# Three main steps instead of two behind each small product in the mixer of a two-layer RWKV and pooling trunk

## The chip, the cores and the metric

The kernel runs on one core of one Trainium2 chip. The metric is the device time of one execution in microseconds (us), as the median of the runs shown. A profile of one further execution gives every instruction's start and duration on each engine: PE (TensorE, matrix products), DVE (VectorE), ACT (ScalarE), POOL (GpSimd) and SP (SyncE, which here only issues transfers).

## The reference

A prompt of 256 tokens and a sample group of 8 x 4 tokens (288 columns in all) pass through two layers that share all weights. Each layer is an FFN, a mixer and a second FFN. Cut to what matters:

```
for l in range(2):
    x = x + 0.5 * gate * swiglu(norm(x))                  # FFN, 1024 -> 2 x 2816 -> 1024
    p = u @ w_in[l]                                       # 19 column tiles of 128
    ya, state = rwkv7(p[:, :1824], ...)                   # S = S*w + (S a) b + v k ; y = S r ; group norm, gate
    yb = pool(p[:, 1824:], windows 2, 4, 8, 16) @ w_pool  # causal means less the input, one product for each window
    merged = sig(u @ w_gate_a) * (ya @ w_br_a) + sig(u @ w_gate_b) * (yb @ w_br_b)
    x = x + gate * (merged @ w_out)
    x = x + 0.5 * gate * swiglu(norm(x))                  # second FFN
y = final_norm(x)
```

The recurrence of the prompt is computed in chunks of 64 tokens: products of all token pairs inside a chunk ("scores"), the solution of a triangular system, and four chunk states one after the other. The 8 samples bring their own states, which are read, used and written back.

## The kernel before

Every large product runs in float32 precision as three passes of a rounded format: `mm3` (L244) multiplies the high part of the weights with the high and the low part of the activations, and the low part of the weights with the high part. One pass is a 128x128 weight block against 288 columns. For four weight blocks at a time ACT writes the high part `wh` (L225) and DVE the low part `wl` (L226); four such strips of `wh` and `wl` are held. All passes of `mm3` are tied to each other in the order of the code.

The mixer (`mixer`, from L623) has two streams of work on PE. The first are the **main passes**: `main_ops` goes through the column tiles of the list `MAIN` (the input projection `in`, the gate `ga` for pooling's branch), then pooling's branch product `bb` and the second half of `ga`. It is a generator: one **step** is two weight blocks, six passes. There are 22 x 4 steps for `MAIN`, 8 x 2 for `bb` and 8 x 4 for `ga`, 136 in all. The second stream are the **small products** of the recurrence, which wait for DVE and ACT between one another. `add` puts a small product into a queue with `WEAVE` steps behind it, and `fill()` takes the next number of `PLAN` and pops that many entries; where the queue is empty it makes plain steps:

```
def add(*items):
    for f in items:
        queue.extend((f,) + WEAVE * (step,))
def fill(n=None):
    for _ in range(next(plan, 2) if n is None else n):
        (queue.popleft() if queue else step)()
```

The mixer calls `fill()` once for each number of `PLAN`, in this order: seven times up to the scores (products L906, masked on DVE in L910); then a queue of 13 small products is added (`bonus`, eight transpositions into token order, `values`, `ak_v`) and `fill()` is called four times around the triangular system, whose DVE part ends in the tile `Tc` (L1172) and whose first product is L1179; the rest of the queue is emptied. Then nine products of the samples are added (among them `smp_state`, L1042, four times: each reads 256 KB of state into the one buffer of tag `O0` through a transfer on ACT's queue, and multiplies it, L1048), and `fill()` is called twice for each of the four chunks. In the second chunk eleven more are added: `spread_bonus` and `out_gate` twice each, `outputs(0)`, `smp_last(0)`, `smp_yt`, `transposed(0)`, `smp_last(1)`, `(2)`, `(3)`. `smp_last` (L1144) reads a state into the buffer `O0` again (ACT's queue), adds a product (L1152) to it on DVE (L1154), scales it on POOL (L1155) and writes it out on SP's queue. After the chunks come `outputs(1)`, a `fill()`, the rest of the queue, and `transposed(1)`: four transpositions on PE (L1238) and four DVE operations (L1141, L1142). The result `xv` is then split into `yah` (ACT, L522) and `yal` (DVE, L523) for four tiles with a `fill()` behind each, which are plain steps; `need(99)` makes the steps that are left. Then comes the product `ba`, whose first column tile needs all of `yah` and `yal`.

Pooling: `pooled` builds `dd` (its last operation is L695) on DVE, and `pool_out` (L704) multiplies it by the pooling weights (L706) and splits the result (`ybh` on ACT, `ybl` on DVE, L709). Each `dd` has one of two buffers. `pool_out` and the main passes take their PSUM tiles from the same three, `psmm`; the other small products take theirs from four others, `pswk`.

When the program is built, the instructions of each engine are put into a fixed order by priority (the order of the code, with a lead of 75 for the weights and some main results) and by when their inputs are reckoned to be ready. So the order on PE need not be that of the queue: where a small product is not ready, main passes that stand later in the code come first. It keeps the order in which the tiles of one PSUM pool are taken.

Of the kernel before, what the change touches and what calls it, by code (L numbers as in the profile page):

```python
# [27 lines left out]
KD = 8  # L28
# [37 lines left out]
TOK = (0, P, NT - P)  # L66
SLOT = 8
PRIO = 75
WEAVE = 2
PLAN = (1, 0, 0, 11, 1, 15, 12, 16, 5, 6, 2, 0, 10, 12, 2, 2, 1, 8, 13, 1, 2, 8, 4, 2, 3, 0, 5, 1, 1, 7)  # L70
FIRST = 3
RMS = {0: 0.25, 1: 0.15, 2: 0.25}
SPREAD = {0: 0.45, 1: 0.4, 2: 0.45}
# [115 lines left out]
class Kernel:  # L189
# [433 lines left out]
    def mixer(self, l):  # L623
# [7 lines left out]
        def tl(shape, tag, name=None, dt=F32, bufs=1):  # L631
            return pl.tile(shape, dt, tag=tag, name=name or tag, bufs=bufs)

        def f4(tag, name=None, dt=F32):
            return tl([P, HP, NT], tag, name, dt)
# [68 lines left out]
        def pool_out(g, dd):  # L704
            ps = self.ps_mm()
            T.matmul(ps[:, :NT], wpl[:, g, :], dd, start=True, stop=True)  # L706
            sc = self.par(l, "pool_scale", g)
            S.activation(out=ybh[:, g, :], in_=ps[:, :NT], func=AF.Copy, scale=sc)
            V.scalar_tensor_tensor(out=ybl[:, g, :], in0=ps[:, :NT], scalar=sc, in1=ybh[:, g, :].bitcast(F32),  # L709
                                   op0=ALU.mult, op1=ALU.subtract)  # L710

        dds = {}

        def project(m, ps):
            name, i = IN_TILES[m]
            if name == "la":
                shifted(i, ps, xla)
                S.activation(out=xla[0:64, :], in_=xla[0:64, :], func=AF.Tanh)
            elif name in "krv":
                shifted(i, ps, {"k": xk, "r": xr, "v": xv}[name][:, i % 4, :])  # L720
            elif name == "gl":
                shifted(i, ps, sgl[:, i - 13, :])
                S.activation(out=sgl[:, i - 13, :], in_=sgl[:, i - 13, :], func=AF.Sigmoid)
            else:
                dds[i - 15] = pooled(i - 15, ps)

        def project_pre(m, ps):
            p = p0[:, m % KD, :]
            c = self.scaled(ps, p, V)
            V.tensor_scalar(p[:, :TP], p[:, :TP], c, None, op0=ALU.add)  # L730
            project(m, p)

        def strip(name, m, n=KD, xh=None, xl=None, w=NT):
            xh, xl = (self.uh, self.ul) if xh is None else (xh, xl)
            ps = self.ps_mm()
            for k in range(n):
                self.mm3(ps[:, :w], (name, l, 0, m, k), xh[:, k, :], xl[:, k, :], k == 0, k == n - 1)
                if k % 2:
                    yield ps
# [3 lines left out]
        def main_ops():  # L743

            for n, (name, m) in enumerate(MAIN):
                pre = name == "in" and m < PRE_M
                for ps in strip(name, m, xh=self.vh, xl=self.vl, w=NV) if pre else strip(name, m):
                    yield n
                if (name, m) == ("in", PRE_M - 1):
                    self.v_cm.__exit__(None, None, None)  # L750
                with tc.high_priority(offset=PRIO):
                    if pre:
                        project_pre(m, ps)
                    elif name == "in":
                        project(m, ps)
                    else:
                        S.activation(out=t2s[0][:, m - KD, :], in_=ps[:, :NT], func=AF.Sigmoid,
                                     bias=self.par(l, "b_gate", m))
                if name == "in" and m == 14:
                    nc.sync.dma_start(out=self.io["o_shift"][l], in_=sho)  # L760
                if name == "in" and m == 14:
                    t2s.append(tl([P, KD, NT], "t2"))
                if name == "ga":
                    if m - KD - 2 in dds:
                        pool_out(m - KD - 2, dds[m - KD - 2])
                    self.mod_step()
            at_bb = len(MAIN)
            for m in range(KD):
                for ps in strip("bb", m, 4, ybh, ybl):
                    yield at_bb  # L770
                with tc.high_priority(offset=PRIO):
                    V.tensor_tensor(out=t2s[0][:, m, :], in0=t2s[0][:, m, :], in1=ps[:, :NT], op=ALU.mult)
            gA.extend([f4("ybh", "gA0"), f4("ybl", "gA1")])
            for m in range(KD):
                for ps in strip("ga", m):
                    yield at_bb + 1
                with tc.high_priority(offset=PRIO):
                    gate = S.activation(out=gA[m // 4][:, m % 4, :], in_=ps[:, :NT], func=AF.Sigmoid,
                                        bias=self.par(l, "b_gate", m))
                if m == KD - 1:  # L780
                    self.table(AF.Sqrt, gate)
                self.mod_step()
            while True:
                yield 99
# [3 lines left out]
        ybl = f4("ybl", dt=F32R)  # L788
        gA = []
        main = main_ops()  # L790
        at = [-1]
        queue, plan = deque(), iter(PLAN)

# [7 lines left out]
# [5 lines that stand above are left out]
# [685 lines left out]
```

## Time and profile before

| | before |
|---|---|
| median of 3 runs | 1428.73 us (1427.41 to 1429.08) |
| the profiled execution's own time | 1431.08 us |
| span of the profiled execution | 1429.3 us |
| mean granted TensorE clock | 0.993 |
| PE busy | 1383.5 us (97%) |
| DVE busy | 960.1 us (67%) |
| ACT busy | 722.6 us (51%) |

The span runs from the first to the last instruction. The two mixers lie from about 262 to 504 us and from about 961 to 1203 us. A row of the timeline gives start, duration, engine, line, operation, output and inputs, and in brackets how long the engine had been idle before it and what ended that.

### The profile page before, as it was taken

How to read it: one execution, taken by the hardware profiler on the slowest of the kernel's cores; microseconds unless marked ns; L12 is line 12 of the kernel's file. 1: busy time of each engine (PE TensorE's matmuls, PEld its weight loads, DVE VectorE, ACT ScalarE, POOL GpSimd, SP SyncE). 2: the span in 40 equal slices, each digit the busy share in tenths (PEclk: the TensorE clock that was granted, in tenths of full speed). 3: DMA queues.
4: the chain of work that ended last, by engine and by line, in shares of the span. 5: the costliest groups of instructions: out<-in, count | busy, mean ns of one | idle time of the engine just before them, and what ended most of it. 6: DMA issues, size and time to landing. Idle time of an engine off the chain costs nothing.

```text
span 1429.3 us, 28790 instructions
## 1 busy us (share of the span) xinstructions
PE 1383.5 (97%) x11280; PEld 1282.7 (90%) x11280; DVE 960.1 (67%) x2065; ACT 722.6 (51%) x1460; POOL 108.4 (8%) x151
## 2 busy tenths in 40 slices
PE   6999999999999999999999999999999999999997
PEld 5989999988778999899999999998887899999997
DVE  4645556899766895455667555669996778755554
ACT  4544444675424665444455445448653356555532
POOL 0000002000022010000211000120001200100012
PEclk9999999999999999999999999999999999999999
DMA  8878864443325676787667645454342257445452
GB/s 362 319 269 304 298 249 167 153 142 112 113 66 171 243 268 223 269 303 264 245 246 251 253 149 163 163 175 140 113 139 90 93 185 268 160 163 163 164 170 98
DMA packets 72568, 281.84 MB, mean 197 GB/s; under 512 B 9584, under 2 KB 11760, under 8 KB 63088
## 3 DMA queue, kind: packets, MB, share of 16 engines
q1 hardware_dynamic: 66384, 272.24, 54.4%
q10 hardware_dynamic: 6048, 7.77, 1.8%
q8 instruction: 88, 1.44, 0.4%
q14 instruction: 48, 0.39, 0.1%
HBM read 275.74 MB, written 4.23 MB: 196 GB/s over the span
## 4 chain that ended last, share of the span: by engine, by line
PE 83%; DVE 8%; DMA 3%; issue 2%; ACT 2%; POOL 1%; POOLq 0%; DVEq 0%; ACTq 0%; SPq 0%
PE psmm L251 42%; PE pswk L251 31%; PE psmd L315 4%; DVE wl L226 2%; DMA s<-in_wkv 2%; POOL gn L1110 1%; PE pswk L1048 1%; PE pswk L918 1%; DMA raw<-in_wflat 1%; DVE MM L910 1%; PE pswk L1256 0%; ACT wh L225 0%; PE pswk L814 0%; DMA cc<-in_c 0%; PE pswk L1128 0%
## 5 line engine op out<-in xcount | busy, mean ns | idle before, releaser
L226 DVE TENSOR_TENSOR wl<-raw,wh 128x512 fp32r<-128x512 f32 x732 | 513.3, 704 | 331.0 <-ACT wh L225 322.0
L225 ACT CAST wh<-raw 128x512 fp32r<-128x512 f32 x732 | 452.7, 620 | 550.9 <-PE psmm L251 285.5
L251 PE MATMUL psmm<-uh,wl 128*128 128x288 f32 x1072 | 318.4, 297 | 4.3 <-DVE wl L226 4.3
L251 PE MATMUL psmm<-uh,wh 128*128 128x288 f32 x1072 | 319.8, 298 | 2.2 <-ACT uh L506 2.2
L251 PE MATMUL psmm<-ul,wh 128*128 128x288 f32 x1072 | 318.2, 297 | 0.6 <-DVE ul L507 0.3
L251 PEld LDWEIGHTS psmm<-uh,wh 128*128 128x128 f32 x1072 | 202.1, 188 | 11.3 <-issue 5.1
L251 PEld LDWEIGHTS psmm<-uh,wl 128*128 128x128 f32 x1072 | 202.1, 189 | 9.4 <-DVE wl L226 5.7
L251 PEld LDWEIGHTS psmm<-ul,wh 128*128 128x128 f32 x1072 | 202.0, 188 | 3.6 <-issue 1.7
L251 PE MATMUL pswk<-ul,wh 128*128 128x288 f32 x608 | 179.6, 295 | 0.0
L251 PE MATMUL pswk<-uh,wh 128*128 128x288 f32 x608 | 179.5, 295 | 0.0
L251 PE MATMUL pswk<-uh,wl 128*128 128x288 f32 x608 | 179.5, 295 | 0.0
L251 PEld LDWEIGHTS pswk<-uh,wh 128*128 128x128 f32 x608 | 114.7, 189 | 5.4 <-issue 4.2
L251 PEld LDWEIGHTS pswk<-ul,wh 128*128 128x128 f32 x608 | 114.6, 189 | 0.0
L251 PEld LDWEIGHTS pswk<-uh,wl 128*128 128x128 f32 x608 | 114.5, 188 | 0.0
L251 PE MATMUL pswk<-hl,wh 128*128 128x288 f32 x352 | 103.8, 295 | 0.0
L251 PE MATMUL psmm<-hl,wh 128*128 128x288 f32 x352 | 103.8, 295 | 0.0
L251 PE MATMUL psmm<-hh,wl 128*128 128x288 f32 x352 | 103.8, 295 | 0.0
L251 PE MATMUL pswk<-hh,wl 128*128 128x288 f32 x352 | 103.7, 295 | 0.0
L251 PE MATMUL psmm<-hh,wh 128*128 128x288 f32 x352 | 103.7, 295 | 0.0
L251 PE MATMUL pswk<-hh,wh 128*128 128x288 f32 x352 | 103.2, 293 | 0.0
L315 PE MATMUL psmd<-modw,csilu 128*32 128x512 f32 (+2 forms) x832 | 69.7, 475 | 9.1 <-DMA modw<-in_wmod 9.1
L378 POOL TENSOR_TENSOR sq<-x 128x288 f32<-128x288 f32 x28 | 19.8, 708 | 769.9 <-DVE x L533 769.9
(321 smaller groups left out, 2388.9 us busy)
## 6 DMA issues: line engine op xcount, KB each, us to landing
raw<-in_wflat SPq DMA_DIRECT2D x366, 512.0 KB, 3.3
modw<-in_wmod SPq DMA_DIRECT2D x72, 1024.0 KB, 7.0
s<-in_wkv ACTq DMA_DIRECT2D x16, 256.0 KB, 3.3
o_wkvs<-s SPq DMA_DIRECT2D x8, 256.0 KB, 2.8
x<-in_x SPq DMA_DIRECT2D x1, 1152.0 KB, 5.4
o_y<-yo SPq DMA_DIRECT2D x2, 288.0 KB, 2.5
o_y<-yo ACTq DMA_DIRECT2D x2, 288.0 KB, 2.6
o_pool<-po SPq DMA_DIRECT2D x8, 67.5 KB, 3.0
```

Source lines behind the costliest of these rows:

```text
L225: self.nc.scalar.copy(wh, src)
L226: self.nc.vector.tensor_tensor(out=wl, in0=src, in1=wh.bitcast(F32), op=ALU.subtract)
L251: self.last = self.nc.tensor.matmul(ps, w, x, start=start and n == 0, stop=stop and n == 2)
L315: mm = nc.tensor.matmul(self.mod_ps[32 * q:32 * q + 32, :size], self.csilu[:, k, :], w[:, kk, q, :], start=(k == 0), stop=(k == KD - 1))
L378: nc.gpsimd.tensor_tensor(out=t, in0=x, in1=x, op=ALU.mult)
L910: V.tensor_tensor(out=MM[:, 2 * e + i, :, q].rearrange("p h x t -> p h (x t)"), in0=pss[e].rearrange("p (h y) -> p h y", h=HP), in1=maskp, ...
L918: T.transpose(ps[:n, 128 * hp:128 * hp + 128], src(hp), ident)
L1048: T.matmul(ps[halves[e], :], ARs[halves[e], hp].rearrange("p x t -> p (x t)"), s0[halves[e]].rearrange("p b v -> p (b v)"), start=True, st ...
L1110: G.tensor_tensor(out=var, in0=var, in1=self.cst("mhalf", n).to_broadcast([n, nh]), op=ALU.pow)
```

## The change

Three constants or conditions change. `WEAVE` goes from 2 to 3, so that each product of the queue has three steps behind it. Eight numbers of `PLAN` go up: the seventh (steps ahead of the scores) from 12 to 14, the eighth (the first pop of the first queue) from 16 to 18, and six of the pops between the chunks by one or two. And `pool_out(g)` is called after gate tile `KD + 3 + g` instead of `KD + 2 + g`: for windows 0 to 2 that is two column tiles of main passes later (one input tile and one gate tile), for window 3 it is one.

```diff
-WEAVE = 2
-PLAN = (1, 0, 0, 11, 1, 15, 12, 16, 5, 6, 2, 0, 10, 12, 2, 2, 1, 8, 13, 1, 2, 8, 4, 2, 3, 0, 5, 1, 1, 7)
+WEAVE = 3
+PLAN = (1, 0, 0, 11, 1, 15, 14, 18, 5, 6, 2, 0, 12, 13, 4, 4, 3, 9, 13, 1, 2, 8, 4, 2, 3, 0, 5, 1, 1, 7)
...
                 if name == "ga":
-                    if m - KD - 2 in dds:
-                        pool_out(m - KD - 2, dds[m - KD - 2])
+                    if m - KD - 3 in dds:
+                        pool_out(m - KD - 3, dds[m - KD - 3])
                     self.mod_step()
```

## Rows read from the trace of the kernel before

**Rows 1.** The page, part 1: busy time by engine.
```profile
PE 1383.5 (97%) x11280; PEld 1282.7 (90%) x11280; DVE 960.1 (67%) x2065; ACT 722.6 (51%) x1460; POOL 108.4 (8%) x151
```

**Rows 2.** Waits of PE over the whole span: total us, times, longest.
```profile
PE psmm L251 <- DVE wl L226: 6.3, 6, 1.8
PE psmm L706 <- DVE dd L695: 4.7, 4, 1.4
PE pswk L1048 <- DMA s<-in_wkv: 3.3, 3, 1.9
PE pswk L906 <- DVE AR L888: 3.2, 2, 1.6
```

**Rows 3.** Stretches, first mixer: length, busy PE, PEld, DVE, ACT, POOL, clock, DMA.
```profile
280.00:327.30 47.30, 44.60 (x337) 38.69 (x337) 46.43 (x121) 33.53 (x78) 0.00 (x0) 1.00 0.40 129
327.30:368.30 41.00, 37.28 (x262) 33.80 (x262) 37.76 (x113) 25.76 (x55) 1.27 (x4) 1.00 0.42 133
...
439.40:465.70 26.30, 24.40 (x181) 23.74 (x180) 16.02 (x26) 12.43 (x26) 2.87 (x3) 1.00 0.60 191
478.40:503.90 25.50, 25.50 (x195) 25.50 (x194) 21.37 (x63) 16.64 (x37) 0.00 (x0) 1.00 0.80 300
```

**Rows 4.** Timeline of DVE: a weight split and pooling's split, first mixer.
```profile
316.53 0.68 DVE L226 TENSOR_TENSOR wl<-raw,wh 128x512 fp32r<-128x512 f32 x1
...
364.19 0.52 DVE L709 SCALAR_TENSOR_TENSOR ybl<-psmm,par,ybh 128x288 fp32r<-128x288 f32 x1
```

**Rows 5.** Timeline of PE up to the triangular system's first product.
```profile
362.86 0.51 PE L706 MATMUL psmm<-dd,wpl 128*128 128x288 f32 x1 [1.36 <-DVE dd L695]
...
368.35 0.82 PE L1179 MATMUL pswk<-Tc,MM 32*32 32x32 f32 x40 [0.25 <-DVE Tc L1172]
```

**Rows 6.** Timeline of PE: a product of the samples' states, second mixer.
```profile
1087.70 1.08 PE L1048 MATMUL pswk<-s,ARs 64*64 64x512 f32 x4 [1.94 <-DMA s<-in_wkv]
```

**Rows 7.** Stretches with like work in both mixers, two pairs: length, PE busy, clock, DMA.
```profile
405.79:416.51 10.72, 10.72 (x41) 0.68 0.01 2
1107.37:1114.92 7.55, 7.55 (x41) 1.00 0.01 2
...
387.85:391.31 3.46, 3.46 (x61) 1.00 0.26 80
1088.71:1093.61 4.90, 4.90 (x62) 0.65 0.18 54
```

**Rows 8.** Timeline of PE at and after the last transposition.
```profile
438.83 0.60 PE L1238 MATMUL pswk<-consts,yn 128*128 128x128 f32 x4
439.18 0.38 PE L251 MATMUL psmm<-uh,wh 128*128 128x288 f32 x1
439.40 0.29 PE L251 MATMUL psmm<-ul,wh 128*128 128x288 f32 x1
...
1155.31 0.40 PE L251 MATMUL psmm<-uh,wl 128*128 128x288 f32 x1 [1.76 <-DVE wl L226]
```

**Rows 9.** Timeline of DVE around the last transposition, both mixers.
```profile
437.24 0.68 DVE L1154 TENSOR_TENSOR s<-s,pswk 128x512 f32<-128x512 f32 x1
...
441.16 0.41 DVE L1141 TENSOR_TENSOR ygw<-pswk,gw 128x256 f32<-128x256 f32 x1
...
443.13 0.46 DVE L523 TENSOR_TENSOR yal<-xv,yah 128x288 fp32r<-128x288 f32 x1 [1.10 <-ACT yah L522]
445.70 0.69 DVE L1154 TENSOR_TENSOR s<-s,pswk 128x512 f32<-128x512 f32 x1 [2.11 <-DMA s<-in_wkv]
...
1153.97 0.69 DVE L1154 TENSOR_TENSOR s<-s,pswk 128x512 f32<-128x512 f32 x1 [3.42 <-DMA s<-in_wkv]
```

**Rows 10.** Timeline of POOL ahead of the last transposition, first mixer.
```profile
435.02 1.05 POOL L1149 TENSOR_TENSOR uv<-UVs,consts 128x512 f32<-128x512 f32 x1
```

**Rows 11.** The page, part 6: transfers, size, median us from issue to landing.
```profile
s<-in_wkv ACTq DMA_DIRECT2D x16, 256.0 KB, 3.3
o_wkvs<-s SPq DMA_DIRECT2D x8, 256.0 KB, 2.8
```

## Prediction

> **What bounds the kernel.** I read the busy times first: PE is busy for 97% of the span, so only PE's idle time and what slows its passes can be won, some 46 us in all [rows 1]. The list of PE's waits says where it lies: 6.3 us on weight splits, 4.7 on pooling's `dd`, 3.3 on states from memory, 3.2 on the operand `AR` of the scores [rows 2]. All of the last three are in the mixers, and of the first 4.3 us are (four waits between the last transposition and `ba`; the other two, of 1.0 us each, lie ahead of the change). Third, the stretches of one mixer [rows 3]. From 280 to 327 us DVE is busy for 46.4 of 47.3 us, from 327 to 368 for 37.8 of 41.0: up to `Tc` DVE sets the pace, and PE's idle time is what DVE leaves it. From 439 to 466 it is the other way round: after the last transposition PE has 180 main passes (30 steps), and DVE is idle for 10 us. The last stretch, 195 passes in 25.50 us, gives the price of a main pass: 0.131 us, 0.78 for a step.
>
> **What the queue now does,** counted from the code. Ahead of the scores 1+11+1+15+12 = 40 steps become 42. The first queue has 13 products: 26 steps become 39. The second has 20: 40 become 60. So `transposed(1)` stands behind 106 steps before and behind 141 after. There are only 136. The 106 agree with the 30 steps that the trace shows behind it [rows 3]; after the change none are left, neither for the four splits nor for `need(99)`. This is the other side of the change. Also, in the trace the order is not that of the queue: from 327 to 368 us PE has 262 instructions, of which by the code 38 belong to small products, so 224 passes (37 steps), where the queue asks for 14. Main passes were drawn forward until `Tc` was reckoned ready; there a weave of three changes little. It acts behind `Tc`, where the queue before had been overdrawn by 23 steps and small products stand close together; after it the queue asks for 81 steps by the first chunk and the trace's order has some 40+2+37 = 79, so steps come between products at once.
>
> **The parts, for both mixers together.**
>
> (a) Two steps more ahead of the scores: 12 passes, 1.57 us, in a wait of 1.6 us. They need one more weight split on a DVE that is full, 0.68 us [rows 4], so `AR` comes later by that: 1.6 - 1.57 + 0.68 leaves 0.7, a gain of 0.9 each. -1.8. Ends: 0 (the wait moves on whole) and -3.2 [rows 2].
>
> (b) Pooling's product later: the `dd` waits (the longest 1.36 [rows 5]) go, 4.7 us. But what is late next is `Tc`, for which PE waits only 0.25 us now [rows 5] because it was held up before. DVE needs as long as before, less one `ybl` of 0.52 us [rows 4] that falls behind `Tc`. Unless more passes are drawn forward, PE waits at L1179 for what it no longer waits at L706. I take -1.0; ends 0 and -4.7.
>
> (c) Waits for states: 3.3 us in three, the longest 1.94 [rows 2, 6]. A load takes 3.3 us [rows 11], and behind a product of 1.08 us there will be three or six steps, 2.4 or 4.7 us. I leave 0.6 for the shorter gap: -2.7. Ends 0 and -3.3.
>
> (d) TensorE's clock. The same 41 instructions took 10.72 us in the first mixer at a granted clock of 0.68 and 7.55 in the second at 1.00: 3.2 us. Another stretch took 4.90 at 0.65 in the second and 3.46 at 1.00 in the first: 1.4 us [rows 7]. [...] With three steps behind each product both places hold more passes. 4.6 us are at stake, I take -3.9; ends 0 and -4.6.
>
> (e) The four waits on weight splits behind the last transposition, 4.3 us (the longest 1.76 [rows 8]). They come from `smp_last`: DVE stands in front of L1154 until the state has been loaded, 2.11 and 3.42 us in two of the rows [rows 9], and the splits behind it are late. There are no main passes there any more: -4.3. Ends 0 (they come back in `ba`, see h) and -4.3.
>
> (f) More changes between small products and main passes. The first pass behind a small product takes 0.22 us to the next instead of 0.13 [rows 8]: 0.09 each. Some eight more groups in a mixer: +1.4. Ends 0 and +3.
>
> (g) The bare end. Let E be the end of the last main pass. `smp_last(3)` has one step between it and `smp_last(2)`, and its operand takes POOL 1.05 us [rows 10] after that product, against 0.78: +0.3. Then come the transpositions, 0.60 us [rows 8], four DVE operations of 0.41 and four `yal` of 0.46, less some 0.08 by which neighbours overlap [rows 9]: about 0.6+1.3+1.5 = 3.4, then the last passes of `ba`'s first tile, 0.5. By then this tile would have been done in 0.35+1.57 = 1.9 without a wait. 3.9-1.9 = 2.0, with the 0.3: 2.3 in each mixer, +4.6. Ends +3 (`yah` and `yal` overlap better) and +7.
>
> (h) DVE's queue there. From the start of `smp_last(1)`'s product to E there are 24 passes and two products of 1.0: 5.3 us. Its add stands at E-4.2; from one such add to the next it took 8.46 us [rows 9], a store and a load of one buffer [rows 11]. So the add of `smp_last(2)` can't run before E+4.2, while the DVE work of (g) is to start at E+1.8. The add comes earlier in the code, and DVE has been seen to stop for such loads [rows 9], so I take it to be ahead of that work. What is queued behind it is the whole chain to `ba`. Price: between 2.11 (the shorter wait seen) and 4.2+0.69-1.8 = 3.1 us; I take 2.4 each, +4.8. Ends 0 (the add is placed behind `yal`) and +6.8, two waits of 3.42. The add of `smp_last(3)` then stops DVE in `ba`, where DVE has work for most of the time: like the waits of (e), 1.0 each, +2.0; ends 0 and +3.5.
>
> [...]
>
> (i) New falls of the clock. A wait of 1.94 us stood ahead of one fall [rows 6, 7]; at `Tc` (2 to 3 us, by b) and at E (4 us or more) PE will be idle longer, in four places. Ends 0 and four times 3.2 us, but the work behind E is held by DVE in any case; I take one fall of the smaller kind, +1.4.
>
> Sum: -1.8-1.0-2.7-3.9-4.3 = -13.7, and +1.4+4.6+4.8+2.0+1.4 = +14.2. Together +0.5 us, to the profiled span of 1429.3 (its own time 1431.08 is 2.3 us over the median of the runs, 0.16%). Put on the median, 1428.73 becomes 1429.2.
>
> **The rivals.**
>
> No change, my forecast: what PE wins in the middle of the mixer it gives back at its end. Within 0.2% (2.9 us, about what can be told apart), 1426 to 1432. Chance 0.36.
>
> Slower: the bare end costs more than the middle gives. The mechanism is (h): DVE and ACT held by state transfers with nothing left on PE. At 3.4 us for the load, 1.7 in `ba` and a clock fall of 1.4 in each mixer, the end costs 2.3+3.4+1.7+1.4 = 8.8 each instead of 2.3+2.4+1.0+0.7 = 6.4: 4.8 more, 1434.0. It decides once an end costs over 7.6 us. For it: in the code the adds of `smp_last(2)` and `(3)` stand ahead of the splits, and PE has no cover. Against it: in (e) the same stops cost PE at most 1.76 us. Chance 0.32.
>
> Faster, by the end: the add of `smp_last(2)` is placed behind the splits, (h) falls to 2.0: 1424.4. For it: in the trace `yal` of the first tile ran ahead of such an add [rows 9]. Chance 0.19.
>
> Faster, by pooling: without L706 in front more passes are drawn ahead of `Tc` and (b) gives 4.7: 1425.5, and 1424.1 if (i) is gone with it. Against it: DVE is full there. Chance 0.13.
>
> That the change does nothing it says is excluded for the end and is so, as shown, for the stretch ahead of `Tc`.
>
> **Numbers.** The likeliest case gives 1429.2. The range takes the slower case with a further fall of the clock in each mixer, 1438, and the faster ones where two of them meet, 1422. Faster 0.31, same 0.36, slower 0.33.
>
> **What would show it.** PE's first `ba` pass waits 4 to 6 us on `yal` (2 to 2.5 if h is wrong), with an L1154 waiting for a load just ahead on DVE. L706 waits for nothing, and L1179 waits 2 us or more on `Tc`; if it doesn't, (b) is wrong and the kernel faster. The wait on `AR` is 0.7. The granted clock near 406 and 1090 us is 1.00; if it is not, (d) is wrong. A clock below 1.00 behind `Tc` or in `ba` is (i).

## The result, and the profile after

| | before | after |
|---|---|---|
| median of 4 runs each | 1428.07 us (1425.43 to 1429.08) | 1444.36 us (1443.62 to 1447.04) |
| the profiled execution's own time | 1431.08 us | 1443.62 us |
| span of the profiled execution | 1429.3 us | 1441.8 us |
| mean granted clock | 0.993 | 0.984 |

The changed kernel is slower: ratio 1.0113, 95% interval [1.0092, 1.0135]. The prediction said 1429.2 in a range of 1422 to 1438, so both the size and the range are wrong; the span grew by 12.5 us where the sum had 0.5.

First the page, part 1, after the change; it answers to [rows 1]:

```profile
PE 1391.0 (96%) x11280; PEld 1291.0 (90%) x11280; DVE 959.9 (67%) x2065; ACT 724.9 (50%) x1460; POOL 107.2 (7%) x151
```

PE has the same 11280 instructions and is busy 7.5 us longer. So the loss is not in waits alone: some of the same instructions became slower. The list of PE's waits (total us, times, longest), which answers to [rows 2], has the other 5 us:

```profile
PE psmm L251 <- DVE yal L523: 4.0, 2, 2.1
PE pswk L1179 <- DVE Tc L1172: 3.9, 2, 2.0
PE psmm L251 <- ACT yah L522: 3.6, 2, 1.8
PE pswk L1048 <- DMA s<-in_wkv: 3.4, 2, 2.4
PE pswk L906 <- DVE AR L888: 3.2, 2, 1.6
PE psmm L251 <- DVE wl L226: 3.0, 4, 1.0
PE pswk L1152 <- POOL uv L1149: 2.5, 2, 1.3
PE psmm L251 <- DVE gA L1303: 2.5, 2, 1.5
```

L706 is gone from the list and `wl` fell by half; `Tc`, `yal`, `yah`, `uv` and `gA` came; `AR` and `s` are what they were. The stretches of the first mixer (length, busy PE, PEld, DVE, ACT, POOL, clock, DMA; cut at `Tc`, at the chunks' first state product, at the end of the last transposition and at the start of the product `wo`) say where the clock was down:

```profile
327.29:371.45 44.16, 41.54 (x301) 38.24 (x301) 40.83 (x120) 27.86 (x59) 1.27 (x4) 1.00 0.46 146
371.45:386.92 15.47, 15.47 (x302) 13.93 (x303) 5.04 (x13) 8.06 (x14) 1.57 (x3) 0.67 0.16 51
386.92:464.06 77.14, 73.42 (x699) 59.45 (x695) 51.70 (x103) 26.73 (x54) 14.93 (x15) 1.00 0.34 109
464.06:484.00 19.94, 16.18 (x97) 15.62 (x97) 15.33 (x32) 9.02 (x18) 2.62 (x2) 0.83 0.41 136
...
467.90:474.70 6.80, 6.48 (x25) 6.13 (x26) 3.79 (x8) 0.99 (x2) 1.04 (x1) 0.50 0.23 77
474.70:481.50 6.80, 6.80 (x54) 6.80 (x53) 6.70 (x15) 3.78 (x8) 1.43 (x1) 1.00 0.47 145
372.30:382.50 10.20, 10.20 (x156) 9.06 (x150) 4.21 (x11) 4.57 (x8) 1.57 (x3) 0.50 0.20 61
```

The lowest clock in these rows is 0.50. It is there for 10.2 us right behind `Tc` and for 6.8 us in `ba`. In the second of these, PE got through 25 instructions where it did 54 in the next 6.80 us. The second mixer has the same pair (1078.9 to 1089.1 and 1171.0 to 1177.9). Ahead of each PE had been idle, as the timeline of PE shows (in brackets how long, and what ended it):

```profile
369.18 0.29 PE L251 MATMUL psmm<-uh,wl 128*128 128x288 f32 x1
371.45 1.14 PE L1179 MATMUL pswk<-Tc,MM 32*32 32x32 f32 x56 [1.98 <-DVE Tc L1172]
...
462.40 1.08 PE L1152 MATMUL pswk<-uv,BKTs 64*64 64x512 f32 x4 [1.27 <-POOL uv L1149]
463.41 0.66 PE L1238 MATMUL pswk<-consts,yn 128*128 128x128 f32 x4
465.83 0.40 PE L251 MATMUL psmm<-yah,wh 128*128 128x288 f32 x1 [1.76 <-ACT yah L522]
468.09 0.61 PE L251 MATMUL psmm<-yal,wh 128*128 128x288 f32 x1 [1.86 <-DVE yal L523]
```

The bare end is there as predicted: the last main pass ends at 461.1, then three waits of 1.27, 1.76 and 1.86 us. The timeline of DVE in the same place, answering to [rows 9]:

```profile
459.16 0.67 DVE L1154 TENSOR_TENSOR s<-s,pswk 128x512 f32<-128x512 f32 x1
...
464.10 0.76 DVE L1141 TENSOR_TENSOR ygw<-pswk,gw 128x256 f32<-128x256 f32 x2 [1.21 <-PE pswk L1238]
464.77 0.75 DVE L1142 TENSOR_TENSOR xv<-xv,ygw 128x256 f32<-128x256 f32 x2
466.98 0.69 DVE L1154 TENSOR_TENSOR s<-s,pswk 128x512 f32<-128x512 f32 x1 [1.46 <-DMA s<-in_wkv]
467.59 2.40 DVE L523 TENSOR_TENSOR yal<-xv,yah 128x288 fp32r<-128x288 f32 x4
```

An add of `smp_last` stands in front of all four `yal` and stops DVE for a load: 1.46 us and its own 0.61 to the next, 2.1 us here, and 1.76 + 0.61 = 2.4 in the second mixer. That is the first stop of step (h), at its price of 2.4. The second, of `smp_last(3)`, does not come: DVE reaches that add at 476.72 and 1180.63 us and has no wait there.

### The profile page after: what moved, and what is told of

It is laid out like the page before. It is cut to its first block, busy times and chain, and to the rows that moved or that the text cites. A ratio compares the mean times of both kernels' runs of the same rounds, so it can differ in the third digit from the quotient of the medians.

```text
span 1441.8 us, 28769 instructions
## 1 busy us (share of the span) xinstructions
PE 1391.0 (96%) x11280; PEld 1291.0 (90%) x11280; DVE 959.9 (67%) x2065; ACT 724.9 (50%) x1460; POOL 107.2 (7%) x151
## 4 chain that ended last, share of the span: by engine, by line
PE 90%; DVE 5%; DMA 2%; issue 1%; ACT 1%; POOL 0%; POOLq 0%; DVEq 0%; ACTq 0%
PE psmm L251 47%; PE pswk L251 31%; PE psmd L315 4%; DVE wl L226 1%; DMA s<-in_wkv 1%; PE pswk L918 1%; PE pswk L1048 1%; DVE MM L910 1%; PE pswk L1256 0%; PE pswk L814 0%; DMA cc<-in_c 0%; PE psmm L706 0%; PE pswk L835 0%; PE pswk L977 0%; PE pswk L1204 0%
```

## The experiments

Three explanations stood against each other: the bare end (waits on `yal` and `yah`), the wait that moved from L706 to `Tc`, and the clock, taken to fall where PE stands idle ahead of small products and to slow what follows. The last is the one called C where an expectation uses a letter; other letters are its rivals. The clock column is the median over the runs. The runs come from three chips, so two of them are compared by their ratios to the kernel before on the same chip.

| run | median us (runs) | clock | ratio to before, 95% interval |
|---|---|---|---|
| pooling alone | 1438.01 (9) | 0.986 | 1.0067 [1.0037, 1.0096] |
| weave alone | 1436.71 (5) | 0.993 | 1.0067 [1.0055, 1.0079] |
| two steps ahead of the scores alone | 1437.07 (6) | 0.991 | 1.0078 [1.0062, 1.0093] |
| after, pooling undone | 1438.81 (4) | 0.993 | 1.0068 [1.0041, 1.0094] |
| after, scores' steps undone | 1438.89 (6) | 0.988 | 1.0079 [1.0062, 1.0096] |
| before with a bare end | 1433.99 (10) | 0.994 | 1.0030 [1.0014, 1.0045] |
| after with the end filled | 1441.95 (6) | 0.989 | 1.0084 [1.0058, 1.0111] |
| weave of three at nine products | 1422.30 (5) | 0.998 | 0.9968 [0.9956, 0.9979] |
| pooling later and `Tc` covered | 1416.96 (5) | 0.997 | 0.9934 [0.9922, 0.9947] |
| the last two together | 1414.80 (4) | 0.998 | 0.9903 [0.9885, 0.9922] |

The kernel before, run beside these, had medians of 1426.41 to 1428.35 us at 0.995 to 0.997.

**Pooling alone.** Before, with the one line of pooling changed:

```diff
-                    if m - KD - 2 in dds:
-                        pool_out(m - KD - 2, dds[m - KD - 2])
+                    if m - KD - 3 in dds:
+                        pool_out(m - KD - 3, dds[m - KD - 3])
```

> The kernel before with one part of the change: pooling's products one column tile later. Theory C (the clock: where PE waits in front of small products, TensorE's clock falls, and that costs more than the wait): no waits at L706, a wait of 1 to 2 us at L1179 in each mixer and behind it a clock at the lower level for 3 to 10 us; the 30 steps at the end still stand; 1428 to 1434 us. Theory W (only the waits count): the L706 waits, 2.7 us a mixer, go, 1.7 come at L1179; 1426 us, at most 1428.

Its waits, profiled:

```profile
PE psmm L251 <- DVE wl L226: 6.3, 6, 1.5
PE pswk L1179 <- DVE Tc L1172: 3.6, 2, 1.8
```

L706 is gone from the list and L1179 waits 1.8 us in each mixer. The profiled execution took 1426.59 us at a clock of 0.995; it shows no fall behind `Tc`, and one near 406 (407.6 to 414.4). The other runs of the same program took 1432.1 to 1446.1 us at 0.991 to 0.980 (one more, at 1451.68, over 1.5% above the fastest, is left out of the median and the ratio). So both ranges missed the median; only the profiled execution is where the rival had put it. In that execution the moved wait costs no more than it saves, and the same program takes 5 to 20 us more in runs at a lower clock. Where the clock fell in those runs was not profiled, so that it was behind `Tc` is argued and not shown.

**Weave alone.** Before with `WEAVE` and the pops of the change, but without the two steps ahead of the scores and without the pooling line:

```diff
-WEAVE = 2
-PLAN = (..., 12, 16, 5, 6, 2, 0, 10, 12, 2, 2, 1, 8, ...)
+WEAVE = 3
+PLAN = (..., 12, 18, 5, 6, 2, 0, 12, 13, 4, 4, 3, 9, ...)
```

> The kernel before with the weave of three and the six pops between the chunks (and the first pop of the first queue) of the change, without its steps ahead of the scores and without its pooling part. Theory C (clock and bare end): no clock fall behind L1179, the bare end as in the changed kernel with a fall behind it; 1436 to 1440 us, like the kernel without the pooling part (1438.8), and 3 to 6 us over the bare end alone (1434.0). Theory S (the two steps ahead of the scores, which cut the scores in two, cost the rest): 1434 us.

PE waits 0.4 us at `Tc`, and there are no falls near 406 and 1090, but the bare end is at its worst. The timeline of PE, then that of DVE:

```profile
458.16 0.66 PE L1238 MATMUL pswk<-consts,yn 128*128 128x128 f32 x4
464.61 0.61 PE L251 MATMUL psmm<-yah,wh 128*128 128x288 f32 x1 [5.79 <-ACT yah L522]
```

```profile
462.00 0.69 DVE L1154 TENSOR_TENSOR s<-s,pswk 128x512 f32<-128x512 f32 x1 [1.96 <-DMA s<-in_wkv]
462.61 0.75 DVE L1141 TENSOR_TENSOR ygw<-pswk,gw 128x256 f32<-128x256 f32 x2
```

The last transposition began at 458.16, was done at 458.8, and the DVE work on it stood behind a load until 462.61. The clock is at 0.50 from 463.6 to 470.4 and from 1166.8 to 1170.2. So the weave by itself loses through (g), (h) and the falls behind them, and the time is in the range of C.

**Two steps ahead of the scores alone.** One number of `PLAN`:

```diff
-PLAN = (1, 0, 0, 11, 1, 15, 12, 16, ...)
+PLAN = (1, 0, 0, 11, 1, 15, 14, 16, ...)
```

> The kernel before with only the seventh number of the plan changed, 12 to 14. Theory C: the wait on AR stays at 1.6 us, 12 passes stand between the first and the second part of the scores; no change, 1427 to 1430 us. Theory S: the scores and with them Tc come 1 to 3 us later and PE waits for them: 1431 to 1434 us.

The largest surprise of the study: this part was credited with a gain of 1.8 us and makes the kernel 0.78% slower, more than either range allowed. Its timeline of PE and the list of its waits:

```profile
322.02 1.16 PE L906 MATMUL pswk<-AR,BK 64*128 64x128 f32 x16 [1.62 <-DVE AR L888]
323.69 0.40 PE L251 MATMUL psmm<-uh,wl 128*128 128x288 f32 x1 [0.51 <-DVE wl L226]
...
325.22 1.05 PE L906 MATMUL pswk<-AR,BK 64*128 64x128 f32 x14
...
355.63 0.75 PE L706 MATMUL psmm<-dd,wpl 128*128 128x288 f32 x2 [1.90 <-DVE dd L695]
...
453.00 0.61 PE L251 MATMUL psmm<-uh,wl 128*128 128x288 f32 x1 [2.90 <-DVE wl L226]
```

```profile
PE psmm L251 <- DVE wl L226: 9.9, 7, 2.9
PE psmm L706 <- DVE dd L695: 6.0, 4, 1.9
```

The wait on `AR` is not touched. Behind the first 16 score products PE now has ten main passes in its fixed order, and they wait 0.51 us for a split: the scores are cut in two instead of covered. Then L706 waits 1.9 instead of 1.4 us with a fall behind it (356.8 to 360.2), and at 453 a split comes 2.9 us late, because DVE stands 3.17 us at an add of `smp_last`; there the clock is down from 452.4 to 459.2. The second mixer has one fall, of 3.4 us, near 1164. How two steps at the scores move a state's load at the end wasn't followed further.

**The change with one part undone.** After with the pooling line put back, and after with 12 instead of 14 in the seventh place of `PLAN`:

```diff
-                    if m - KD - 3 in dds:
+                    if m - KD - 2 in dds:
```

> The changed kernel without its pooling part (products where they were before). Theory C: the waits at L706 are back (2.7 us a mixer), the wait at L1179 is small and the clock does not fall behind it; 1434 to 1440 us. Theory W: 5.4 us of waits come back and 3.4 go; 1446 us.

```diff
-PLAN = (1, 0, 0, 11, 1, 15, 14, 18, ...)
+PLAN = (1, 0, 0, 11, 1, 15, 12, 18, ...)
```

> The changed kernel with one number put back: 12 instead of 14 in the seventh place of PLAN (the steps ahead of the scores); the weave of three, the other numbers and the later pooling stay, so the end stays bare. [...] That gives back 2.0 of wait and half of a fall of 10.2 us, 5.1, in each mixer: 1444.4 - 14 = 1430. The end keeps its yal wait of about 2 and its fall of 6.8 to 7.0: no change there. Rival (the end sets it, and what is won earlier only arrives there sooner and waits longer, for DVE and the state transfers): yal or gA wait some 2 us longer, and the time stays at 1440 or over.

With the old pooling the wait at `Tc` is 0.4 us, the stretch behind it runs at full clock, and 1438.81 us remain; the ends keep their waits (`yal` 4.7, `yah` 3.5) and their falls: the mean clock of the profiled execution is 0.993, against 0.997 and 0.998 in those without a fall in a mixer. With the old scores a wait under 0.5 us at L1179 without a fall behind it had been expected, from scores that are not cut in two and a `Tc` that is ready sooner. That missed: the scores are whole again, but L1179 still waits 1.6 and 1.4 us, and the falls behind it are no shorter (372.8 to 386.5 and 1079.4 to 1089.6). From the scores to `Tc` there are 50.1 and 49.9 us, against 50.2 in the changed kernel, so it isn't the cut in the scores that makes `Tc` late. At the end PE waits 11.0 us on `yah` and 0.9 on `gA`, in all about as long as the changed kernel with its 12.6 on `yal`, `yah`, `uv` and `gA`. The stretches behind `Tc`, first of after with the old pooling, then of after with the old scores:

```profile
369.25:382.31 13.06, 13.00 (x307) 11.27 (x308) 7.33 (x17) 8.86 (x16) 1.73 (x3) 1.00 0.25 88
```

```profile
371.74:389.23 17.49, 17.49 (x304) 15.26 (x305) 5.72 (x14) 9.06 (x16) 1.72 (x3) 0.61 0.20 66
```

Like work takes 13.0 us at full clock, 15.5 in the changed kernel at 0.67, 17.5 here at 0.61. What comes with the later `Tc` is seen on DVE, in the groups of its instructions from the scores to `Tc` (busy us, mean ns), first before, then after:

```profile
L226 DVE TENSOR_TENSOR wl<-raw,wh 128x512 fp32r<-128x512 f32 x21 | 14.3, 682 | 0.7 <-ACT wh L225 0.7
...
L688 DVE TENSOR_TENSOR pw<-px 128x422 f32<-128x422 f32 x3 | 1.8, 588 | 0.0
L688 DVE TENSOR_TENSOR pw<-pw 128x420 f32<-128x420 f32 (+1 forms) x3 | 1.8, 586 | 0.0
```

```profile
L226 DVE TENSOR_TENSOR wl<-raw,wh 128x512 fp32r<-128x512 f32 x24 | 16.2, 682 | 1.6 <-ACT wh L225 1.6
...
L688 DVE TENSOR_TENSOR pw<-pw 128x420 f32<-128x420 f32 (+2 forms) x6 | 3.5, 582 | 0.0
L688 DVE TENSOR_TENSOR pw<-px 128x422 f32<-128x422 f32 x4 | 2.4, 592 | 0.0
```

Three more splits (1.9 us) and four more sums of pooling (2.3 us) run ahead of `Tc`. DVE is busy there for 46.8 us instead of 43.8 and idle for 3.3 as before (3.2), so the stretch from the scores to `Tc` grew from 47.0 to 50.2 us by DVE's work. That it is these two groups alone is argued: the run with the old scores has 23 splits and needs 50 us, the covered run below has 22 and needs 48.3, both with the four sums more. PE got 262 passes for that stretch instead of 224, and still waits 2 us.

**A bare end in the kernel before.** The steps that are left are made ahead of the last transposition instead of behind it:

```diff
+        need(99)
         transposed(1)
```

> The kernel before with one line more: all main steps that are left are made ahead of the last transposition instead of behind it. Nothing else moves, so the difference is the price of the bare end. Theory C: waits of 5 us on yah, yal and the last states' operand, less the 2.2 us of waits on weight splits that go, and a clock fall of 6.8 us behind them, 3.4 us more; 5 to 7 us a mixer, 1438 to 1442 us, the old falls near 406 and 1089 us still there. Theory W: the waits alone, 3 us a mixer, 1434 us.

Slower by 0.30%, as the rival had it (the waits alone, 1434 us); C with its 1438 to 1442 missed. PE waits 2.4 us on `yah` in each mixer, and a fall of 3.4 us follows (465.8 to 469.2, 1165.5 to 1168.9). The waits on `wl` fall only from 6.3 to 3.8. DVE doesn't stop for a load there: its last add of `smp_last` runs at 451.8 and the transposition at 462.5, so this run prices (g) without (h), and (g) had 2.3 us a mixer. Such an end explains about a quarter of the change's 1.13%; the changed kernel's own end, with the stop and the longer falls, is not priced by it.

**The changed kernel with its ends filled.** 28 passes that nothing reads stand between the last transposition and `ba`:

```diff
         transposed(1)
+        scrap = self.p_md.tile([P, 512], F32, tag="md", name="scrap")
+        for n in range(28):
+            with tc.issue_after(self.last.ins):
+                self.last = T.matmul(scrap[:, :NT], self.uh[:, n % 8, 0:P], self.ul[:, n % 8, :], start=True, stop=True)
```

> The changed kernel with 28 passes that nobody reads (same form as a main pass, 3.7 us) between the last transposition and ba in each mixer. Theory C: PE's waits there are filled, the clock stays at the upper level behind it, and the time falls by about 3 us a mixer although work was added: 1437 to 1440 us. Theory W: the passes lie in time that was idle anyway; 1444 us, or more by what they hold up.

The falls in `ba` are gone, as the row over most of it in the first mixer shows (clock 1.00):

```profile
469.00:488.00 19.00, 16.94 (x124) 16.22 (x123) 16.56 (x33) 8.05 (x18) 2.63 (x2) 1.00 0.38 132
```

The passes cost 2 x 28 x 0.131 = 7.3 us, and still the ends are shorter: from the last transposition to the last pass of `wo` 45.2 and 45.4 us instead of 47.1 and 47.5. The median, 1441.95, lies between the two ranges, and its ratio's interval overlaps with that of the changed kernel, so that the whole got faster is not shown. The falls behind `Tc` stay; the mean clock of the profiled execution is 0.988. One pair of rows of this run and of the changed kernel shows how loosely a fall hangs on its wait. First after, then this run, the same product behind the same load:

```profile
397.38 1.08 PE L1048 MATMUL pswk<-s,ARs 64*64 64x512 f32 x4 [2.44 <-DMA s<-in_wkv]
398.38 0.40 PE L251 MATMUL psmm<-ybh,wh 128*128 128x288 f32 x1
```

```profile
397.67 1.97 PE L1048 MATMUL pswk<-s,ARs 64*64 64x512 f32 x4 [2.35 <-DMA s<-in_wkv]
399.57 0.61 PE L251 MATMUL psmm<-ybh,wh 128*128 128x288 f32 x1
```

With 2.44 us of idleness the clock held, with 2.35 us it fell (396.9 to 403.8) and the product took 1.97 instead of 1.08 us.

**The wait at `Tc` covered.** Pooling alone, and 30 steps of main passes made right ahead of L1179, which the next 30 steps of the queue then leave out:

```diff
+        debt = [0]
         def step():
+            if debt[0]:
+                debt[0] -= 1
+                return
             at[0] = next(main)
+        def ahead(n, owed):
+            for _ in range(n):
+                at[0] = next(main)
+            debt[0] += owed
...
         fill()
+        ahead(30, 30)
         ps = self.ps_wk()
```

> The kernel before with the pooling part of the change, and with 18 more main passes placed ahead of L1179 (the same number is left out of the steps behind it, so that the end is as before). Theory C: waits at L706 gone, the wait at L1179 under 1 us, no clock fall behind it: 1422 to 1427 us, where the pooling part alone took 1439.7. Theory T (it is not the wait but the later place of the four pooling products among the small ones that costs): 1436 to 1440 us as with the pooling part alone.

PE has 262 passes ahead of `Tc` here too, 16 more than with pooling alone, and with 22 splits instead of the 24 of the changed kernel. L1179 (L1190 in this kernel) waits for nothing, the profile has no fall in either mixer, and the mean clock is 0.997 to 0.998 in all runs. By the two ratios, 1.0067 and 0.9934, this is 1.3% faster than pooling alone, some 19 us, and below the 1422 that C had as its least. The rival, that the later place of pooling's products costs, is out: they stand as late here.

**A weave of three at the nine products of the samples only,** with the pops between the chunks raised and everything else as before:

```diff
-PLAN = (..., 0, 10, 12, 2, 2, 1, 8, ...)
+PLAN = (..., 0, 12, 13, 4, 4, 3, 8, ...)
...
-                queue.extend((f,) + WEAVE * (step,))
+                queue.extend((f,) + (3 if len(items) == 9 else 2) * (step,))
```

> The kernel before with three steps behind the nine products of the samples alone; 21 of the 30 steps behind the last transposition stay. Theory C: the states' waits get shorter, the falls near 406 and 1089 us do not come, the end stays covered: 1422 to 1427 us. If the weave itself costs (more changes between products and passes), 1429 to 1432 us.

Faster by 0.32%: 21 steps are left for the end, and the falls near 406 and 1089 don't come. This is the part of the change that did what (c) and (d) had hoped. Of its 4.1 us little can be the clock: the kernel before ran beside it at 0.997 and this one at 0.998, which is 1.4 us at most by an estimate (0.001 of 1426). The waits are the larger part: those on `wl` fall from 6.3 to 4.4 us, those on a state's load from 3.3 to 0.2, with 1.9 new on `shs` at the same product.

**Both together.** The edits of the last two runs in one kernel:

> The kernel before with three pieces: pooling's products one column tile later, main passes drawn forward ahead of the triangular system's first product (as in the covered run, 262 passes between scores and Tc), and a weave of three behind the nine products of the samples alone, with the pops raised for them. [...] Rival: both win the same thing, a mixer without a fall of the clock, and it can be had once: 1416 to 1418. A further rival: the steps owed after Tc leave the nine products bare all the same, and the ends get fewer steps: over 1418, with waits of 1 us or more on yal.

1414.80 us, 0.97% faster than before and the best of all. By the ratios the gains add in full: 0.9934 x 0.9968 is 0.9902, and 0.9903 was measured; 0.9934, the rival's "had once", lies outside the interval. The theory that the gains add had put them as 1417.0 - 5.8 = 1411. That was too low because its 5.8 is 1428.07 less 1422.30, and the kernel before had 1426.41 on that run's chip. Both mixers, from the product ahead of the scores to the end of `wo`:

```profile
282.30:496.39 214.09, 207.62 (x1904) 183.79 (x1905) 179.69 (x445) 119.77 (x257) 20.36 (x24) 1.00 0.44 149
973.76:1186.90 213.14, 207.66 (x1904) 183.75 (x1905) 179.26 (x445) 120.23 (x257) 20.34 (x24) 1.00 0.45 152
```

No fall in either. PE is busy 207.6 us for its 1904 instructions, which is the price of a mixer at full clock.

## Why the prediction was wrong

The mixers by the same cut, the second one before and after:

```profile
981.84:1203.00 221.16, 210.38 (x1904) 185.30 (x1905) 179.58 (x445) 120.43 (x257) 20.78 (x24) 0.99 0.44 146
```

```profile
987.61:1215.13 227.52, 214.55 (x1904) 189.19 (x1905) 179.41 (x445) 121.57 (x257) 20.52 (x24) 0.96 0.43 143
```

The first went from 221.96 (PE busy 212.08) to 228.81 (214.99 busy). Together the mixers grew by 13.2 us, 7.1 of it busy and 6.1 idle; the rest of the span lost 0.7. The terms, with what the rows of the two profiles have in their place:

| step | predicted | measured | from |
|---|---|---|---|
| (a) wait on `AR` | -1.8 | +1.0 | 3.2 to 3.2, and 2 x 0.5 new on `wl` between the scores |
| (b) pooling | -1.0 | -1.3 | `dd` -4.7, `Tc` 0.5 to 3.9 |
| (c) states | -2.7 | +0.1 | 3.3 to 3.4 |
| (e) splits at the end | -4.3 | -4.3 | 4.3 to 0.0 (in all 6.3 to 3.0, with the 1.0 of (a)) |
| (g), (h) bare end | +11.4 | +12.6 | `yal` 4.0, `yah` 3.6, `uv` 2.5, `gA` 2.5 |
| smaller waits | 0 | -2.0 | the rest of the idle time |
| (d) old falls | -3.9 | -4.6 | no fall near 406, none of the old kind near 1090 |
| (i) new falls | +1.4 | +11.4 | 2 x 2.4 behind `Tc`, 2 x 3.3 in `ba` |
| (f) switches | +1.4 | +0.3 | the rest of the busy time |
| sum | +0.5 | +13.2 | |

For (i), 2.4 is 15.47 less the 13.06 that like work takes at full clock, and 3.3 is 6.48 less what 25 instructions take at 54 in 6.80 us. The second mixer's are put at the same; its fall in `ba` has 21 instructions in 5.45 us of busy time, which by the same working is 2.8, so 11.4 is some 0.5 high.

**The step that failed is (i).** It named the right four places and the upper bound held the answer (four times 3.2), but it took one fall of the smaller kind, +1.4, on the ground that the work behind the end is held by DVE in any case. Four came, 10.2 us long behind each `Tc` and 6.8 and 6.9 in `ba`. Behind `Tc` that ground didn't apply. In `ba` it held in part: PE had 25 passes to do in 6.8 us and did them at half speed, but in the run with filled ends, at full clock, PE waits on DVE there once more (0.54 and 0.56 us on `yal` in the first mixer). The same 289 instructions from the first pass on `yal` to the end of `wo` took 42.8 and 42.8 us after the change and 40.3 and 40.6 with the ends filled. So a fall in `ba` cost some 2.3 us of time, and (i) some 9.4 in all instead of 1.4: 8.0 of the 12.7 us by which the sum missed, or 10.0 by the table. The rival that forecast a slower kernel, at 1434.0, had falls at the ends only; those behind `Tc` it left out.

**Second, (a) and (c).** The wait on `AR` stayed, because the extra passes were put behind the first score products and waited 0.51 us for their own split there (at 322.95 and 1028.38); the sum assumed that steps ahead in the code are ahead in PE's order, which the rows of before had already contradicted for `Tc`. For (c) the load behind the wait of 2.44 us was issued at 391.9 and its product began at 397.4: 5.5 us, where (c) had counted on 3.3, and PE's other work covered 3.1 of them. With the old pooling the changed kernel has no wait on a state left, so the steps can cover a load; why this one took longer is open. Together the two missed by 5.6 us.

**(b) had about the right size by a wrong reason.** DVE was said to need as long as before, less one `ybl`. It is busy for 3.0 us more, with what was drawn forward, and `Tc` is 3.1 us later after the scores. PE's 38 further passes make it busy for 4.1 us more in that stretch (42.7 to 46.8), which doesn't cover both this and L706's old waits (2.7 us in a mixer), and 2.0 us of wait stand at `Tc`.

**(g) and (h) were right in place and order, and in size partly by luck.** The wait on `uv` is 1.27 us where (g) had 0.3, 2.5 us of waits on `gA` stand in `wo`, and the 2.0 that (h) had for the stop of `smp_last(3)` did not come. The median load of the changed kernel took 3.2 us and the median store 2.3, against 3.3 and 2.8 before; from one add of `smp_last` to the next there were 7.8 and 8.1 us, where (h) had counted on 8.46.

**(d) was right for the profile, not for the median.** Those falls were in the profiled execution, at a clock of 0.993. The median clock of its 21 runs beside pooling alone was 0.997, and 0.004 of 1429 us more is, by an estimate, some 11 us less at a clock of 0.50, about as long as both old falls together (6.9 and 3.4 us). So the usual run had little there to win; that it lacks just these falls is argued, as it was not profiled. That more main passes in the two places would hold the clock up was the author's estimate.

What stays open: why the three parts, each slower by 0.67 to 0.78% alone, make 1.13% together, and why a wait of like length is followed by a fall in one run and not in the next. No run has the changed kernel with both `Tc` covered and its ends filled, so what the two would give back together is not shown.

## What to carry to other kernels

Fillers are worth where they cover a wait, not by their count: three behind each product used up the steps that covered the end, while the same steps moved ahead of `Tc`, or put behind nine products only, made the kernel 0.3 to 1.0% faster (the first together with the later pooling). Before a wait is moved or a tail is left bare, price it twice: by its length, and by what can follow it at a clock of 0.50 (6.8 to 10.2 us at a time in the changed kernel). And where passes are drawn forward, count what they bring to the engine that sets the pace: with three splits and four sums more, `Tc` came 3.1 us later, most of the 4.1 us of work that PE gained.

## What the runs showed of the hardware

One program on one chip: pooling alone took 1426.59 us at a mean granted clock of 0.995 and 1446.12 at 0.981. The kernel before, in 21 runs beside it, spread from 1425.04 to 1433.32. Waits of 1.4 to 2.0 us at L1179 were followed by falls of 10.2 to 13.7 us in the traces of after, of after with its end filled and of after with the old scores, and by none in that of pooling alone at 1.8 us. What sets the moment of a fall is not shown by any run here.

The falls behind `Tc`, where small products follow, lasted 10.2 to 13.7 us; those in `ba`, where main passes follow, 3.4 to 6.9. And a fall need not have a wait ahead of it: in the profile of before, the fall at 406 us came after a stretch of mostly small products in which PE was hardly idle (from 398 to 406 us its longest wait was 0.17).
